# Two of each FFN tile's four weight sums made ahead in DRAM by copies and adding transfers, and loaded

## The chip, the cores and the metric

The kernel runs on one core of a Trainium2 chip. Its time is the device time of one execution in microseconds, as the median of several runs. The engines are named as in the profile: PE is TensorE (matmuls, with PEld for its weight loads), DVE is VectorE, ACT is ScalarE, POOL is GpSimd, SP is the engine that issues most DMA transfers.

## The reference

A trunk of two layers on 512 tokens with D = 1024. Layer 0 mixes with HGRN2 (a gated linear recurrence, evaluated in chunks), then one shared key and value are projected, and layer 1 mixes with chunked band attention. Each mixer is followed by a SwiGLU FFN with 2816 hidden columns. The shift, scale and gate of each step come from a conditioning vector c. The parts that matter here:

```
mod = c_act @ mod_w[layer] + mod_b[layer]
sh1, sc1, g1, sh2, sc2, g2 = jnp.split(mod, N_MOD, axis=-1)
...
u = modulate(rms_norm(h, norm_ffn[layer]), sh2, sc2)
gate, up = jnp.split(u @ w_in, 2, axis=-1)
h = h + g2[:, None, :] * ((jax.nn.silu(gate) * up) @ w_out)
```

## The kernel before, in words

**Numbers.** Everything is fp32. A product of two fp32 matrices is made as three matmuls on halves: each operand is split into a high part (a rounded copy, made on ACT) and a low part (operand minus high part, on DVE); high·high, high·low and low·high are added up in PSUM (mm3, L203 to L205). The low part of a weight is sometimes made by an adding transfer of POOL instead (L144).

**Weights.** `weight_plan` lists all weight pieces, mostly 512 KB, in the order of use. `load` (L159) issues them on SP into three buffers called raw, two pieces ahead of use; `split` (L130) makes the halves, `take` (L192) hands a raw piece out unsplit. Loads on SP are issued in program order, and one that waits for its buffer holds back those behind it.

**The fast tiles.** The FFN's inner columns are 22 tiles of 128 gate and 128 up columns. Tiles 0 to 3 are plain matmuls. Tiles 4 to 21 of both layers go through `fast_tiles` (L532): the 2×2 block product (inner index in even and odd k-tiles, tokens in halves of 256, gate beside up) is made with seven products instead of eight, each of 4 k-tiles × 3 matmuls, so 84 matmuls of 128x256 a tile, on L575 to L577. Their left operands are sums of the weight blocks. The blocks come in two loads, c1 with b11 and b21, c2 with b22 and b12. `prepare(n)` (L544) makes on DVE t1 = b12 − b11 (L554), t2 = b22 − t1 (L555), t3 = b22 − b12 (L558) and t4 = b21 − t2 (L559), in the tiles x1 (t2, t1) and x2 (t3, t4). `halves` (L537) splits them: ACT makes the high part (L540), DVE the low one (L541), for w1 (from c1), w2 (x1), w3 (x2) and w4 (b22 alone). In the profile the loads are `r_f_c`, the sums `f_x`, the halves `f_w_h` and `f_w_l`, the products `f_r`. The preparation of a tile runs while PE works on the tile before it. In tiles 8, 12, 16 and 20, and 4, w4 stands shifted in its buffer.

The input sums, on the tokens' side, are made once per layer in `fast_inputs` (L398 to L414). The seven products are combined on ACT and DVE (L598 to L617) into gate and up, and their product `f_ar` is the tile's result. Later it is split for the output projection (L491/L492 in layer 0, L650/L652 and L687/L688 in layer 1), into places that become free; a list `room` sets which.

**Beside them.** `mod_vectors` (L328) makes the modulation vectors as row reductions on DVE: 512 KB loads `mw` (L342), one instruction L353 each, woven into the mixers and into two of three fast tiles. On POOL stand a few instructions of the normalizations, `ors` (L1095) of the HGRN mixer among them, whose results its chain of DVE and PE waits for; kq (L990) and oe (L1101) are DVE's steps in that mixer that PE waits for.

**Order.** Each engine works through its own list in order; the list of each is laid out when the kernel is built, and places in SBUF that are used again make the waits.

Of the kernel before, what the change touches and what calls it, by code (L numbers as in the profile page):

```python
# [41 lines left out]


FAST = (0, 1)
PLAIN = 4


CUT, MEAN_AT, WRITE_AT = 256, 5, 11
# [26 lines left out]
def trunk(ctx: ExitStack, tc: tile.TileContext, d, out):  # L75
# [295 lines left out]
    def fast_inputs(fp, rb, a, sh, nm):  # L371

        H = S // 2
        his = [fp.tile([P, 8, H], F32R, tag=f"uo{j}", name=f"{nm}_h{j}") for j in range(KT // 2)]
        los = [[cst.tile([P, 2, H], F32R, tag=f"u{'hl'[q % 2]}{2 * j + q // 2}", name=f"{nm}_l{j}_{q}", bufs=1)
                for q in range(4)] for j in range(KT // 2)]
        xs = [fp.tile([P, 4, 2, H], F32, tag=f"xs{g}", name=f"{nm}_x{g}") for g in range(2)]
        ss = [fp.tile([P, 4, 2, H], F32, tag=f"xs{2 + g}", name=f"{nm}_s{g}") for g in range(2)]  # L380

        s1 = cst.tile([P, KT // 2], F32, tag=f"{nm}_sh1", name=f"{nm}_sh1")
        sp = sh.rearrange("p (j e) -> p j e", e=2)
        V.tensor_add(s1, sp[:, :, 0], sp[:, :, 1])
# [12 lines left out]

        def sums(g, late):  # L398
            x, y = xs[g], ss[g]
            if not late:  # L400
                V.tensor_add(y[:, 0], x[:, 0], x[:, 2])
                V.tensor_sub(y[:, 1], y[:, 0], x[:, 1])
                for j in (2 * g, 2 * g + 1):
                    for q, b in ((0, s1[:, j:j + 1]), (1, sh[:, 2 * j + 1:2 * j + 2])):
# [5 lines left out]
            V.tensor_sub(y[:, 3], x[:, 3], y[:, 1])  # L410
            for j in (2 * g, 2 * g + 1):
                v, u_ = y[:, 2:4, j % 2, :], his[j][:, 6:8, :]
                A.activation(u_, v, AF.Copy)
                V.tensor_sub(los[j][3], v, u_)  # L414

        return his, los, sums

    def ffn(layer, z0, u, g2, side, finish):
        nm = f"f{layer}"
        fast = layer in FAST  # L420
        with tc.tile_pool(name=nm, bufs=1) as fp:
# [3 lines left out]
            if fast:  # L425
                his, los, sums = fast_inputs(fp, *u, nm)

                def slot(j, s):
# [2 lines left out]
                u = [(his[k // 2][:, 2 * (k % 2):2 * (k % 2) + 2, :].rearrange("p a c -> p (a c)"),  # L431
                      los[k // 2][k % 2].rearrange("p a c -> p (a c)")) for k in range(KT)]

            def activated(n):

                if not fast or n == FT - 1:
                    return sm.tile([P, S], F32, tag="sq", name=f"{nm}_at{n}", bufs=2)

                g, e = divmod(n, 2) if n < FIRST else divmod(n - FIRST, 4)
                if e == 0:  # L440
                    tag, m = (f"ab{g}", 2) if n < FIRST else (f"xs{g}", 4)
                    raw_a[n] = fp.tile([P, m, S], F32, tag=tag, name=f"{nm}_ar{n}")
                return raw_a[n - e][:, e, :]
# [4 lines left out]
            for n in range(PLAIN if fast else FT):  # L448
                sg = sm.tile([P, S], F32, tag="ut", name=f"{nm}_s{n}", bufs=2)
                at = activated(n)  # L450
                if n == 0:
                    (tg, bg), (tu, bu) = z0
                    A.activation(sg, tg, AF.Silu, bias=bg)
                    V.scalar_tensor_tensor(at, tu, bu, sg, op0=ALU.add, op1=ALU.mult)
                else:
                    res = []
                    drain(proj((nm, n, 0), u, res))
                    if not fast:
                        next(side, None)
# [7 lines left out]
                    V.tensor_mul(at, res[1], sg)  # L467
                kept(n, at)
                if fast and n in (1, 2):
                    sums(0, n == 2)  # L470
            if fast:
                fast_tiles(fp, nm, slot, activated, kept, side)
            if layer == OUT:
                drain(side)
                fast_out(fp, nm, a, raw_a, FIRST, g2, finish)
# [53 lines left out]
                    later = finish(n, c)  # L529
            drain(side)  # L530

    def fast_tiles(fp, nm, slot, activated, kept, side):  # L532

        H = S // 2
        ops = {}
# [1 line left out]
        def halves(key, raw, n_, at=NEAR):  # L537
# [3 lines left out]
            V.tensor_sub(wl, raw, wh)  # L541
            return [(wh[:, i], wl[:, i]) for i in range(n_)]

        def prepare(n):  # L544
# [4 lines left out]
            x1 = fp.tile([P, 2, 4, P], F32, tag="x1", name=f"{m}_x1")  # L549
            x2 = fp.tile([P, 2, 4, P], F32, tag="x2", name=f"{m}_x2")  # L550
# [3 lines left out]
            V.tensor_sub(t1, b12, b11)  # L554
            V.tensor_sub(t2, b22, t1)  # L555
            yield
            ops[n, 6], ops[n, 5] = halves(f"{m}_w2", x1, 2)
            V.tensor_sub(t3, b22, b12)  # L558
            V.tensor_sub(t4, b21, t2)  # L559
            yield  # L560
            ops[n, 7], ops[n, 4] = halves(f"{m}_w3", x2, 2)
            yield
            ops[n, 3], = halves(f"{m}_w4", c2[:, 0:1], 1, NEAR if (n - PLAIN) % EVERY else APART)
            yield
# [64 lines left out]
    def fast_out(fp, nm, a, raw_a, first, g2, finish):  # L629
# [3 lines left out]
        K0 = 2 * PAIRS  # L633
        halves = (slice(0, CUT), slice(CUT, S))
        room = [(cst, f"ul{i}", 1) for i in range(8)] + [(cst, "uh4", 1), (cst, "uh5", 1)]
        room = [(fp, f"sp{i}", 1) for i in range(10)] + room + [(fp, "sp10", 1), (cst, "uh6", 1), (cst, "uh7", 1)]
        room += [(mp, "mraw", 2), (mp, "mraw", 2), (mp, "crow", 2), (fp, "xs1", 4), (fp, "xs0", 4), (sm, "et", 1)]
        units = []

# [124 lines left out]
                T.matmul(ps, wl[:, j, :], uh, start=False, stop=j == PAIRS - 1, skip_group_check=True)  # L764

        def onto(n, c, ps):
            g = ng2 if n % 2 else g2
            V.scalar_tensor_tensor(h[n][:, c], ps, g[:, n:n + 1], h[n][:, c], op0=ALU.mult, op1=ALU.add)

        ng2 = cst.tile([P, KT], F32, tag="a_kv", name="ng2")  # L770
# [53 lines left out]
        for c, ns in zip(halves, (HELD[::-1], HELD)):  # L824
            for n in ns:
                ps = bank(f"{nm}_o{n}_{c.start}h")
                for ci in range(2):
                    for kt in range(CHUNK):
# [993 lines left out]
```

## Time and profile before

| what | value |
|---|---|
| median of 3 runs | 1219.13 us (1218.88 to 1219.14) |
| the profiled execution | 1219.44 us, its span 1217.7 us |
| granted TensorE clock | 0.999 |
| DMA, mean over the span | 151 GB/s, 183.62 MB |
| fast tiles, first matmuls of tile 4 and of the tile after 21 | layer 0 about 340 to 514 us, layer 1 about 920 to 1094 us |

How to read the rows: a row of a group has line, engine, operation, out<-in with buffer numbers left out, shapes and count, then busy us and mean ns of one, then the idle time of the engine just ahead of it and what ended it. A row of a timeline begins with start and duration in us; square brackets hold idle time ahead of it and what ended it. Busy matmuls are pipelined, so the distance of two starts, not the duration, is what one costs. The layer 0 mixer fills about 100 to 300 us, the attention about 640 to 880 us.

### The profile page before, as it was taken

Reading aid. Unit: us, or ns where it says so; the run is one execution under the profiler, and the core shown is the slowest. Engines: PE = TensorE matmul, PEld = TensorE weight load, DVE = VectorE, ACT = ScalarE, POOL = GpSimd, SP = SyncE. Lnnn points to the kernel's source line nnn. Section 1 sums busy time; section 2 is a strip of 40 time slices with the busy share of each in tenths; the row PEclk is TensorE's granted clock in tenths of the full one; section 3 lists DMA queues with packets and bytes.
Section 4 is the critical chain, followed back from the end, with each engine's and each line's share of the span. In section 5 each row is a group of like instructions: output and inputs, shape, how many; then the busy total and the mean of one; then the engine's idle time right before and its main releaser. Section 6 shows DMA issues by size and latency. Waiting matters only on the chain.

```text
span 1217.7 us, 22201 instructions
## 1 busy us (share of the span) xinstructions
PE 1200.7 (99%) x8758; PEld 1052.3 (86%) x8758; DVE 1027.6 (84%) x1860; ACT 668.7 (55%) x1194; POOL 32.0 (3%) x41
## 2 busy tenths in 40 slices
PE   8999999999999999999999999999999999999997
PEld 7887788788899999988888877777889999998997
DVE  8997778977989999987668879996797999988985
ACT  6455446343656666742228556675465566665452
POOL 0100000000000000000000000000000000001100
PEclk9999999999999999999999999999999999999999
DMA  9632354463424444468752444431333344346842
GB/s 358 255 128 98 111 185 150 154 217 121 108 101 139 156 153 143 155 205 278 239 179 83 135 139 138 160 132 36 121 87 121 122 153 148 118 115 155 218 122 91
DMA packets 55992, 183.62 MB, mean 151 GB/s; under 512 B 6352, under 2 KB 8784, under 8 KB 55888
## 3 DMA queue, kind: packets, MB, share of 16 engines
q1 hardware_dynamic: 53584, 175.65, 42.6%
q0 software_dynamic: 2304, 6.55, 3.2%
q8 instruction: 68, 1.11, 0.4%
q14 instruction: 36, 0.29, 0.1%
HBM read 176.68 MB, written 2.10 MB: 147 GB/s over the span
## 4 chain that ended last, share of the span: by engine, by line
PE 84%; DVE 8%; ACT 3%; issue 2%; DMA 2%; POOL 0%; DVEq 0%; POOLq 0%; ACTq 0%
PE f_r L577 9%; PE f_r L575 9%; PE f_r L576 9%; PE f_o L204 4%; PE f_o L205 4%; PE f_o L203 3%; PE f_or L764 1%; PE o L1087 1%; PE f_or L762 1%; PE f_or L763 1%; PE bo L1499 1%; PE bo L203 1%; PE av L226 1%; PE f L205 1%; PE bo L205 1%
## 5 line engine op out<-in xcount | busy, mean ns | idle before, releaser
L577 PE MATMUL f_r<-f_h,f_w_l 128*128 128x256 f32 x1008 | 279.2, 277 | 0.5 <-DVE f_w_l L541 0.5
L575 PE MATMUL f_r<-f_h,f_w_h 128*128 128x256 f32 x1008 | 279.2, 277 | 0.1
L576 PE MATMUL f_r<-f_l,f_w_h 128*128 128x256 f32 x1008 | 279.0, 277 | 0.0
L577 PEld LDWEIGHTS f_r<-f_h,f_w_l 128*128 128x128 f32 x1008 | 189.3, 188 | 0.9 <-DVE f_w_l L541 0.9
L576 PEld LDWEIGHTS f_r<-f_l,f_w_h 128*128 128x128 f32 x1008 | 189.7, 188 | 0.1
L575 PEld LDWEIGHTS f_r<-f_h,f_w_h 128*128 128x128 f32 x1008 | 189.3, 188 | 0.4 <-ACT f_pu L603 0.3
L353 DVE SCALAR_TENSOR_TENSOR mw<-mw,crow 128x1024 f32<-128x1024 f32 x96 | 115.5, 1220 | 0.5 <-DMA mw<-in_modw 0.5
L540 ACT ACTIVATE f_w_h<-f_x 128x1024 fp32r<-128x1024 f32 x72 | 76.8, 1066 | 45.9 <-PE f_r L576 38.9
L541 DVE TENSOR_TENSOR f_w_l<-f_x,f_w_h 128x1024 fp32r<-128x1024 f32 x72 | 88.0, 1224 | 5.9 <-ACT f_w_h L540 3.2
L540 ACT ACTIVATE f_w_h<-r_f_c 128x1024 fp32r<-128x1024 f32 x72 | 61.2, 849 | 42.4 <-PE f_r L576 39.8
L139 ACT ACTIVATE f_o_h<-r_f_o 128x1024 fp32r<-128x1024 f32 (+2 forms) x39 | 34.4, 892 | 77.0 <-PE f_o L204 56.7
L541 DVE TENSOR_TENSOR f_w_l<-r_f_c,f_w_h 128x1024 fp32r<-128x1024 f32 x72 | 68.7, 954 | 6.0 <-ACT f_w_h L540 6.0
L204 PE MATMUL f_o<-f_p,f_o_h 128*128 128x512 f32 x176 | 68.6, 390 | 0.2 <-DVE f_p L492 0.2
L205 PE MATMUL f_o<-f_p,f_o_l 128*128 128x512 f32 x176 | 68.7, 390 | 0.0
L203 PE MATMUL f_o<-f_p,f_o_h 128*128 128x512 f32 x176 | 68.4, 389 | 0.0
L146 DVE TENSOR_TENSOR f_o_l<-r_f_o,f_o_h 128x1024 fp32r<-128x1024 f32 (+2 forms) x35 | 36.1, 1036 | 21.2 <-ACT f_o_h L139 20.0
L1474 ACT ACTIVATE sb<-sb,st 128x128 f32<-128x128 f32 (+1 forms) x64 | 35.9, 561 | 29.9 <-DVE st L1473 29.4
L204 PEld LDWEIGHTS f_o<-f_p,f_o_h 128*128 128x128 f32 x176 | 33.0, 188 | 7.4 <-DVE f_p L492 0.6
L205 PEld LDWEIGHTS f_o<-f_p,f_o_l 128*128 128x128 f32 x176 | 33.0, 188 | 7.3 <-DVE f_o_l L146 0.6
L203 PEld LDWEIGHTS f_o<-f_p,f_o_h 128*128 128x128 f32 x176 | 33.0, 188 | 6.8
L990 DVE TENSOR_TENSOR kq<-kq,t 128x1024 f32<-128x1024 f32 x28 | 34.2, 1223 | 5.1 <-PE fine L1014 2.4
L205 PE MATMUL f<-f_h,f_l 128*128 128x512 f32 x96 | 36.9, 391 | 0.3 <-DMA f_l<-r_f 0.3
(515 smaller groups left out, 3216.2 us busy)
## 6 DMA issues: line engine op xcount, KB each, us to landing
mw<-in_modw SPq DMA_DIRECT2D x96, 512.0 KB, 4.2
r_f_c<-in_ffn_in SPq DMA_DIRECT2D x72, 512.0 KB, 3.3
mrow<-in_modw SPq DMA_DIRECT2D x16, 512.0 KB, 8.1
r_f<-in_ffn_in SPq DMA_DIRECT2D x16, 512.0 KB, 3.3
r_f_o<-in_ffn_out SPq DMA_DIRECT2D x16, 512.0 KB, 3.9
r_f_o<-in_ffn_out SPq DMA_DIRECT2D x16, 320.0 KB, 3.0
r_f_o_c<-in_ffn_out SPq DMA_DIRECT2D x12, 384.0 KB, 4.0
r_av<-in_a_v SPq DMA_DIRECT2D x8, 512.0 KB, 3.9
```

Source lines behind the costliest of these rows:

```text
L139: A.activation(wh, raw, AF.Copy)
L146: low = V.tensor_sub(wl, raw, wh)
L203: T.matmul(ps, wh[:, kt, :], uh, start=start, stop=False)
L204: T.matmul(ps, wh[:, kt, :], ul, start=False, stop=False)
L205: T.matmul(ps, wl[:, kt, :], uh, start=False, stop=stop)
L353: V.scalar_tensor_tensor(mw, mw, 1.0, crow, op0=ALU.mult, op1=ALU.mult, accum_out=raw[:, j:j + 1])
L540: A.activation(wh, raw, AF.Copy)
L541: V.tensor_sub(wl, raw, wh)
L575: T.matmul(ps, wh[:, j, :], uh, start=f, stop=False, skip_group_check=True)
L576: T.matmul(ps, wh[:, j, :], ul, start=False, stop=False, skip_group_check=True)
L577: T.matmul(ps, wl[:, j, :], uh, start=False, stop=stop and j == 3, skip_group_check=True)
L1474: A.activation(s[:, 0:n], s[:, 0:n], AF.Exp, bias=st[:, 1:2], accum_out=st[:, 2:3])
```

## The change

A pool in DRAM is added, and a generator `add_up` that makes two sums per fast tile there: b11 + b12 and b22 + b12. For every two tiles SP copies b11 (then b22) of both from the weights to the new place, 512 KB from DRAM to DRAM, and POOL adds b12 of both onto it with an adding transfer, issued one copy later. One copy goes out with two of three weight loads, from the first load of the gates in layer 0 and of the queries in layer 1 on; 18 copies and 18 adds per layer. In the fast tiles each sum is loaded (256 KB) to where t1 and t3 stood, one tile ahead; even tiles use the places sp0 and sp1, odd ones x1 and x2. DVE makes t2 and t4 only. As the sums have plus signs, t1 and t2 turn their sign against before, and with them the second column and row of the block product: the input sums change signs, and so do the gate g2 in the output (or its negative is used) and the results of the plain tiles. Since sp0 and sp1 are now taken in the fast tiles, the lists of places for the split results are rearranged. Matmuls are the same, one for one, in the same order.

```diff
+    dp = ctx.enter_context(tc.tile_pool(name="dp", bufs=1, space=bass.MemoryType.DRAM))
...
             key, src, nk, n_ = plan[state["loaded"]]
+            for layer, name in enumerate(("g", "bq")):
+                if key[0] == name and layer not in adding:
+                    adding[layer] = add_up(layer)
+            if state["loaded"] % 3:
+                for layer in adding:
+                    next(adding[layer], None)
...
+    def add_up(layer):
+        last = None
+        for b in range(FT - PLAIN)[::BATCH]:
+            for i in range(2):
+                t = dp.tile([P, BATCH, 4 * P], F32, tag=f"t{layer}{b}{i}", name=f"ws{layer}_{b}_{i}")
+                w = d["ffn_in"][layer, PLAIN + b:PLAIN + b + BATCH].rearrange("n v p k c -> v p n (k c)")
+                with tc.issue_after(state["asked"].ins):
+                    nc.sync.dma_start(t, w[i, :, :, 0:4 * P])
+                for e in range(BATCH):
+                    sums_at[layer, PLAIN + b + e, i] = t[:, e, :]
+                if last:
+                    G.dma_start(out=last[0], in_=last[1], accum_op=ALU.add)
+                last = t, w[1, :, :, 4 * P:8 * P]
+                yield
+        G.dma_start(out=last[0], in_=last[1], accum_op=ALU.add)
...
+            if fast and layer != OUT:
+                V.tensor_scalar_mul(g2, g2, -1.0)
...
+                    if fast:
+                        V.tensor_scalar_mul(at, at, -1.0)
...
+        def summed(n):
+            for k in (n, n + 1):
+                if k < FT and k not in asked:
+                    x = [fp.tile([P, 2, 4, P], F32, tag=(f"x{i + 1}", f"sp{i}")[k % 2 == 0], name=f"{nm}_{k}_x{i + 1}") for i in range(2)]
+                    for i in range(2):
+                        nc.sync.dma_start(x[i][:, 1 - i].rearrange("p j c -> p (j c)"), sums_at[layer, k, i])
+                    asked[k] = x
+            return asked.pop(n)
...
-            V.tensor_sub(t1, b12, b11)
-            V.tensor_sub(t2, b22, t1)
+            V.tensor_add(t2, b22, t1)
             yield
             ops[n, 6], ops[n, 5] = halves(f"{m}_w2", x1, 2)
-            V.tensor_sub(t3, b22, b12)
-            V.tensor_sub(t4, b21, t2)
+            V.tensor_add(t4, b21, t2)
...
-        room = [(fp, f"sp{i}", 1) for i in range(10)] + room + [(fp, "sp10", 1), (cst, "uh6", 1), (cst, "uh7", 1)]
+        room = [(fp, f"sp{i}", 1) for i in range(2, 9)] + [(fp, "sp0", 2), (fp, "sp1", 2)] + room + [(cst, "uh6", 1), (cst, "uh7", 1)]
```

On DVE, in layer 1 while PE works on tile 6 (`f_6`: halves of tile 6, `f_7_x`: sums of tile 7), there stands before:

```order
L541 TENSOR_TENSOR f_6_w_l<-f_6_x_9908,f_6_w_h 128x1024
L617 TENSOR_TENSOR f_ar_9693<-f_ar_9693,f_qu_9842 128x256
L554 TENSOR_TENSOR f_7_x_10037<-r_f_7_c_9906,r_f_7_c_9904 128x512
L541 TENSOR_TENSOR f_6_w_l<-f_6_x_9909,f_6_w_h 128x1024
L555 TENSOR_TENSOR f_7_x_10037<-r_f_7_c_9906,f_7_x_10037 128x512
L558 TENSOR_TENSOR f_7_x_10038<-r_f_7_c_9906 128x512
L559 TENSOR_TENSOR f_7_x_10038<-r_f_7_c_9904,f_7_x_10037 128x512
L541 TENSOR_TENSOR f_6_w_l<-r_f_6_c_9780,f_6_w_h 128x512
```

And after, at the same place (L577 is the old L541, L601 and L604 the two sums left):

```order
L577 TENSOR_TENSOR f_6_w_l<-f_6_x_9903,f_6_w_h 128x1024
L577 TENSOR_TENSOR f_6_w_l<-f_6_x_9904,f_6_w_h 128x1024
L662 TENSOR_TENSOR f_ar_9810<-f_ar_9810,f_qu_9963 128x256
L601 TENSOR_TENSOR f_7_x_10029<-r_f_7_c_10027,f_7_x_10029 128x512
L604 TENSOR_TENSOR f_7_x_10030<-r_f_7_c_10025,f_7_x_10029 128x512
L577 TENSOR_TENSOR f_6_w_l<-r_f_6_c_9901,f_6_w_h 128x512
```

Two sums are gone, and the low half of tile 6's w3 (`f_6_w_l<-f_6_x_9904`) no longer stands behind a sum that reads tile 7's c2.

On POOL, in the HGRN mixer, there is before only this around the first two normalizations:

```order
L1337 MEMSET ad 128x1024
L973 MEMSET af_1384 128x256
L1095 TENSOR_TENSOR ors_1294<-oms_1292,nhalf 128x8
L973 MEMSET af_1889 128x256
L1095 TENSOR_TENSOR ors_1805<-oms_1803,nhalf 128x8
```

And after, with the adds (`ws_0_0` is the first sum of tiles 4 and 5, `ws_0_1` the second):

```order
L1382 MEMSET ad 128x1024
L188 DMA ws_0_0_1358<-in_ffn_in 256x1x512
L1018 MEMSET af_1388 128x256
L188 DMA ws_0_1_1597<-in_ffn_in 256x1x512
L1140 TENSOR_TENSOR ors_1296<-oms_1294,nhalf 128x8
L188 DMA ws_2_0_1716<-in_ffn_in 256x1x512
L188 DMA ws_2_1_1877<-in_ffn_in 256x1x512
L1018 MEMSET af_1902 128x256
L188 DMA ws_4_0_1988<-in_ffn_in 256x1x512
L1140 TENSOR_TENSOR ors_1815<-oms_1813,nhalf 128x8
```

Each normalization now stands behind adds, and each add waits for its copy.

On SP, in the second half of that mixer (`mw` are the loads for the row reductions, `r_ao` those of the output projection), there stands before:

```order
L342 DMA mw_0_2270<-in_modw 128x1024
L342 DMA mw_1_2334<-in_modw 128x1024
L342 DMA mw_2_2357<-in_modw 128x1024
L342 DMA mw_3_2453<-in_modw 128x1024
L342 DMA mw_4_2641<-in_modw 128x1024
L164 DMA r_ao_2647<-in_a_out 128x1024
L164 DMA r_ao_2742<-in_a_out 128x1024
L342 DMA mw_5_2730<-in_modw 128x1024
```

And after:

```order
L184 DMA ws_8_0_2672<-in_ffn_in 256x1x512
L368 DMA mw_0_2289<-in_modw 128x1024
L368 DMA mw_1_2356<-in_modw 128x1024
L368 DMA mw_2_2379<-in_modw 128x1024
L368 DMA mw_3_2475<-in_modw 128x1024
L368 DMA mw_4_2666<-in_modw 128x1024
L171 DMA r_ao_2675<-in_a_out 128x1024
L171 DMA r_ao_2770<-in_a_out 128x1024
L184 DMA ws_8_1_2884<-in_ffn_in 256x1x512
L368 DMA mw_5_2758<-in_modw 128x1024
```

Two copies (`ws`) have come in between, each ahead of a load that one of DVE's reductions waits for.

More of the change, by code (lines that the diff above doesn't have):

```diff
@@ L44 @@
 FAST = (0, 1)
-PLAIN = 4
+PLAIN, BATCH = 4, 2
 CUT, MEAN_AT, WRITE_AT = 256, 5, 11
@@ L165, in load @@
             state["loaded"] += 1
+    sums_at, adding = {}, {}
+    def add_up(layer):
[13 more added lines that the diff above has]
+        G.dma_start(out=last[0], in_=last[1], accum_op=ALU.add)
     def fetch(i, ahead):
@@ L382, in fast_inputs @@
         s1 = cst.tile([P, KT // 2], F32, tag=f"{nm}_sh1", name=f"{nm}_sh1")
+        s2 = sm.tile([P, KT], F32, tag="lbt", name=f"{nm}_sh2")[:, 0:KT // 2]
         sp = sh.rearrange("p (j e) -> p j e", e=2)
-        V.tensor_add(s1, sp[:, :, 0], sp[:, :, 1])
+        V.tensor_sub(s1, sp[:, :, 1], sp[:, :, 0])
+        V.tensor_scalar_mul(s2, sp[:, :, 1], -1.0)
         for k in range(KT):
@@ L400, in sums @@
             if not late:
-                V.tensor_add(y[:, 0], x[:, 0], x[:, 2])
-                V.tensor_sub(y[:, 1], y[:, 0], x[:, 1])
+                V.tensor_sub(y[:, 0], x[:, 2], x[:, 0])
+                V.scalar_tensor_tensor(y[:, 1], y[:, 0], -1.0, x[:, 1], op0=ALU.mult, op1=ALU.subtract)
                 for j in (2 * g, 2 * g + 1):
-                    for q, b in ((0, s1[:, j:j + 1]), (1, sh[:, 2 * j + 1:2 * j + 2])):
+                    for q, b in ((0, s1[:, j:j + 1]), (1, s2[:, j:j + 1])):
                         v, u_ = y[:, q, j % 2, :], his[j][:, 4 + q, :]
@@ L409, in sums @@
             V.tensor_sub(y[:, 2], x[:, 1], x[:, 0])
-            V.tensor_sub(y[:, 3], x[:, 3], y[:, 1])
+            V.scalar_tensor_tensor(y[:, 3], x[:, 3], -1.0, y[:, 1], op0=ALU.mult, op1=ALU.subtract)
             for j in (2 * g, 2 * g + 1):
@@ L466, in ffn @@
                     A.activation(sg, res[0], AF.Silu)
-                    V.tensor_mul(at, res[1], sg)
+                    if fast:
+                        V.scalar_tensor_tensor(at, res[1], -1.0, sg, op0=ALU.mult, op1=ALU.mult)
+                    else:
+                        V.tensor_mul(at, res[1], sg)
                 kept(n, at)
@@ L471, in ffn @@
             if fast:
-                fast_tiles(fp, nm, slot, activated, kept, side)
+                fast_tiles(fp, nm, layer, slot, activated, kept, side)
             if layer == OUT:
@@ L530, in ffn, with fast_tiles @@
             drain(side)
-    def fast_tiles(fp, nm, slot, activated, kept, side):
+    def fast_tiles(fp, nm, layer, slot, activated, kept, side):
         H = S // 2
@@ L542, in halves @@
             return [(wh[:, i], wl[:, i]) for i in range(n_)]
+        asked = {}
+        def summed(n):
[6 more added lines that the diff above has]
+            return asked.pop(n)
         def prepare(n):
@@ L548, in prepare @@
             c2 = take((nm, n, "c2")).rearrange("p (o j) c -> p o j c", o=2)
-            x1 = fp.tile([P, 2, 4, P], F32, tag="x1", name=f"{m}_x1")
-            x2 = fp.tile([P, 2, 4, P], F32, tag="x2", name=f"{m}_x2")
+            x1, x2 = summed(n)
             b11, b21, b22, b12 = c1[:, 0], c1[:, 1], c2[:, 0], c2[:, 1]
@@ L766, in onto @@
         def onto(n, c, ps):
-            g = ng2 if n % 2 else g2
+            g = g2 if n % 2 else ng2
             V.scalar_tensor_tensor(h[n][:, c], ps, g[:, n:n + 1], h[n][:, c], op0=ALU.mult, op1=ALU.add)
@@ L784, in fast_out @@
         for n, ps in enumerate(pss):
-            residual(n, ps, g2)
+            residual(n, ps, ng2)
         for n in range(2, HELD[0]):
@@ L796, in fast_out @@
                         ahead((kt + 1) // 2)
-            residual(n, ps, g2)
+            residual(n, ps, ng2)
             if n == MOVED[0]:
@@ L833, in fast_out @@
                         mm3(ps[:, c], ws[n][ci], kt, [x[:, c] for x in a[k]], k == K0, k == FT - 1)
-                residual(n, ps, g2, c)
+                residual(n, ps, ng2, c)
                 later = finish(n, c) or later
```

## The prediction

> **What bounds the kernel now.** I read the page's busy shares first, then its chain, then the rows of the fast tiles, because the change is made for them.
>
> ```profile
> PE 1200.7 (99%) x8758; PEld 1052.3 (86%) x8758; DVE 1027.6 (84%) x1860; ACT 668.7 (55%) x1194; POOL 32.0 (3%) x41
> PE 84%; DVE 8%; ACT 3%; issue 2%; DMA 2%; POOL 0%; DVEq 0%; POOLq 0%; ACTq 0%
> ```
>
> PE is busy for 1200.7 of 1217.7 us and carries 84% of the chain. The change leaves PE's instructions as they are, one for one, so it can only win what PE loses now by waiting or by running slowly. VectorE (DVE), which the change relieves, is second with 84%. The stretches of 20 us in the fast tiles show how near it comes (columns: PE, weight loads, DVE, ACT, POOL, granted clock, DMA share, GB/s):
>
> ```profile
> 380.00:400.00 20.00, 20.00 (x178) 20.00 (x178) 18.87 (x30) 12.41 (x23) 0.00 (x0) 1.00 0.40 137
> 940.00:960.00 20.00, 19.53 (x168) 19.33 (x167) 17.74 (x29) 11.56 (x22) 0.00 (x0) 1.00 0.39 126
> ```
>
> In the first, DVE works 18.87 of 20 us and PE never stops: a full DVE costs nothing as long as it keeps up. Only the second has a hole, of 0.47 us. The list of all that PE waited for says how few holes there are (total us, times, longest):
>
> ```profile
> PE l L1067 <- DVE kq L990: 1.1, 1, 1.1
> PE ot L1110 <- DVE oe L1101: 0.7, 1, 0.7
> PE f_r L577 <- DVE f_w_l L541: 0.5, 1, 0.5
> ```
>
> The first two belong to the HGRN mixer, only the third to the fast tiles: 0.5 us in 3024 matmuls. But PE can be busy and late. Each fast tile is 84 matmuls, so its length is the distance between the starts of its first matmul and of the next tile's. From PE's timeline, the starts of tiles 8, 9, 10, 14, 15 of layer 0, then of tiles 6, 7, 8, 9, 18, 19 of layer 1:
>
> ```profile
> 378.91 0.28 PE L575 MATMUL f_r<-f_h,f_w_h 128*128 128x256 f32 x1
> 388.53 0.28 PE L575 MATMUL f_r<-f_h,f_w_h 128*128 128x256 f32 x1
> 398.05 0.28 PE L575 MATMUL f_r<-f_h,f_w_h 128*128 128x256 f32 x1
> 436.22 0.28 PE L575 MATMUL f_r<-f_h,f_w_h 128*128 128x256 f32 x1
> 446.05 0.28 PE L575 MATMUL f_r<-f_h,f_w_h 128*128 128x256 f32 x1
> ...
> 939.66 0.28 PE L575 MATMUL f_r<-f_h,f_w_h 128*128 128x256 f32 x1
> 950.02 0.28 PE L575 MATMUL f_r<-f_h,f_w_h 128*128 128x256 f32 x1
> 959.91 0.28 PE L575 MATMUL f_r<-f_h,f_w_h 128*128 128x256 f32 x1
> 969.76 0.28 PE L575 MATMUL f_r<-f_h,f_w_h 128*128 128x256 f32 x1
> 1055.71 0.28 PE L575 MATMUL f_r<-f_h,f_w_h 128*128 128x256 f32 x1
> 1065.61 0.28 PE L575 MATMUL f_r<-f_h,f_w_h 128*128 128x256 f32 x1
> ```
>
> An undisturbed tile takes 9.52 us (388.53 to 398.05), one with the shifted w4 9.62 (378.91 to 388.53). Tile 14 of layer 0 takes 9.83. In layer 1 tile 6 takes 10.36, tile 7 9.89, tile 8, which has a shifted w4, 9.85, and tile 18 9.90. So tile 6 stalls, and after it PE goes on at a slower pace, without a hole, until tile 8 is over.
>
> **The change part by part.** It takes t1 and t3 from DVE:
>
> ```profile
> L554 DVE TENSOR_TENSOR f_x<-r_f_c,r_f_c x36: 683/689/693, 334.6 to 1078.0; 128x512 f32<-128x512 f32 x36
> L558 DVE TENSOR_TENSOR f_x<-r_f_c x36: 683/685/691, 335.2 to 1078.7; 128x512 f32<-128x512 f32 x36
> ```
>
> That is 72 × 0.69 = 49 us of DVE's time. Nearly all of it lies beside PE's work, so the gain is not 49 but what the slow tiles lose. Tile 6 of layer 1 shows whether t1 and t3 are on that path:
>
> ```profile
> 943.03 0.69 DVE L554 TENSOR_TENSOR f_x<-r_f_c,r_f_c 128x512 f32<-128x512 f32 x1 [1.92 <-DMA r_f_c<-in_ffn_in]
> 943.64 1.22 DVE L541 TENSOR_TENSOR f_w_l<-f_x,f_w_h 128x1024 fp32r<-128x1024 f32 x1
> ...
> 946.58 0.69 DVE L541 TENSOR_TENSOR f_w_l<-r_f_c,f_w_h 128x512 fp32r<-128x512 f32 x1
> ```
>
> DVE stands 1.92 us for c2 of tile 7, although w3's low half of tile 6 (943.64), which needs no DMA, stands behind that sum. Then come the other sums, and the low half of w4 starts only at 946.58; PE's wait row above names this line. Without t1 and t3 two steps of about 0.60 us (943.03 to 943.64) fall out ahead of it, 1.2 us against a stall of 0.84 (10.36 − 9.52), so the stall goes. The order of after also puts w3's low half ahead of the wait. Next late there is then c2's landing itself, whose sums keep about 0.4 us to spare. With the stall goes the slow pace behind it: tile 7 0.37 (9.89 − 9.52), tile 8 0.23 (9.85 − 9.62). Layer 1 sum: **1.44 us**.
>
> Tile 14 of layer 0 loses 0.31 (9.83 − 9.52). A product split L492 stands there among DVE's rows; it moves to tile 21, since its place sp0 now holds sums, and the two sums ahead go too: **0.31 us**. Tile 18 of layer 1 I leave as it is, since its delay begins on ACT:
>
> ```profile
> 1059.63 0.42 ACT L688 ACTIVATE f_u<-f_ar 128x256 fp32r<-128x256 f32 x1 [0.61 <-DVE mw L353]
> ```
>
> This copy waits for the row reduction L353, and it and another stand ahead of w4's high half on ACT; neither changes its place. The moved splits, three in each layer, each with a copy on ACT like this one:
>
> ```profile
> L491 ACT ACTIVATE f_p<-f_ar x21: 615/623/635, 317.7 to 531.6; 128x512 fp32r<-128x512 f32 x21
> ```
>
> In tiles 20 and 21 their 0.62 us on ACT and 0.69 on DVE cost at least 0, since DVE has two sums less per tile there, and at most one stall like tile 14's in each layer, 0.6 in all; I take 0. The sign turns add one 128x512 multiplication per layer, 0.69 at most like L558, in the plain tiles, hidden by PE: 0, or 0.7 each without that cover.
>
> Then the transfers: 36 copies and 36 adds from DRAM to DRAM, and 72 loads of 256 KB. Before has none of the first two. The nearest rows (KB each, us from issue to landing) and the densest stretch of the HGRN mixer:
>
> ```profile
> mw<-in_modw SPq DMA_DIRECT2D x96, 512.0 KB, 4.2
> r_f_c<-in_ffn_in SPq DMA_DIRECT2D x72, 512.0 KB, 3.3
> f_l<-r_f POOLq DMA_DIRECT2D x4, 512.0 KB, 5.1
> f_t<-in_ffn_out POOLq DMA_DIRECT2D x8, 384.0 KB, 6.7
> ...
> 220.00:250.00 30.00, 28.24 (x371) 22.73 (x371) 24.41 (x38) 13.87 (x39) 1.64 (x1) 1.00 0.55 191
> ```
>
> An add lands after 5.1 (into SBUF) to perhaps 13.4 us (twice the slowest row); I take 6.7, the row with a DRAM addend. The first two adds stand on POOL ahead of the first normalization, and tile 4 first uses their sums where L554 begins now, at 334.6:
>
> ```profile
> 121.70 1.64 POOL L1095 TENSOR_TENSOR ors<-oms,nhalf 128x8 f32<-128x8 f32 x1 [15.26 <-DVE oms L1093]
> ```
>
> So a late add is covered by some 200 us. What is not covered is `ors` behind an add that waits for its copy: POOL is idle 15.26 us before it, the copy ahead of the second add lands in that time; 0, at most the 1.64 of another such instruction. What a copy takes from other transfers: 191 GB/s at a share of 0.55 is 347 GB/s for full engines, so 524288 bytes hold all of them 1.5 us; an add, which reads two and writes one, at most 3.0. In the mixers the weights have two buffers of look-ahead, about 20 us; that covers both. The row reductions' loads have less: 15 of the 36 copies stand on SP directly ahead of one. Now:
>
> ```profile
> L353 DVE SCALAR_TENSOR_TENSOR mw<-mw,crow 128x1024 f32<-128x1024 f32 x96 | 115.5, 1220 | 0.5 <-DMA mw<-in_modw 0.5
> ```
>
> DVE waited 0.5 us for all 96. I take as much again, **+0.5 us**, passed to PE in full; lower end 0 (DVE is idle 5.6 of the 30 us above), upper end in the first rival. By the Trainium skill's page "DMA: Bandwidth & Descriptors", section "Anatomy of one DMA — SWDGE (gpsimd) path", a transfer has about 2.0 us fixed and bytes/436e3 on top, an estimate of 3.2 us for a copy and 1.2 of it on the engines; with that the cost would be 0.4 instead of 0.5. No run here shows a copy from DRAM to DRAM.
>
> In the fast tiles the two sums are asked for one tile ahead, before c1 and c2, when the low halves of w2 and w3 are out; they wait about a tile for their use, and c2 is still the last to land. Cost 0; if they were last, up to 1.9 us per tile as at 943.03.
>
> Sum against the profiled execution of 1219.44: − 1.44 − 0.31 + 0.5 = −1.25, so 1218.2. That execution stands 0.31 above the median of 1219.13, so **1217.9**.
>
> **The rivals.** *Slower: copies in front of the reductions' loads.* DVE takes its instructions in order; an L353 whose load comes late holds back kq (L990) and oe (L1101), the two tiles that PE already waited for. Eight such copies lie in layer 0's mixer. At 1.5 us each they hold DVE 12 us; if half reaches PE, 6.0 − 1.75 = +4.25, or 1223.4. It decides from three copies that reach PE in full: 4.5 − 1.75 = +2.75. For it: the share of 0.55 there. Against it: DVE has waited for these loads once in 96, and has 20% idle. In a sentence of its own: the Trainium skill's page "DMA: Bandwidth & Descriptors", section "Issuing engines are not separate DMA queues", says that transfers of all issuing engines run on the same 16 engines and interleave, so by it the GpSimd adds are no cheaper for these loads than copies on SP; the trace has POOL's 512 KB at 5.1 beside SP's at 3.3, but no two of them together. With the adds as well it would be up to twice, 1229. Chance 0.22.
>
> *No relief: c2 decides.* If c2 lands as late as at 943.03 and its own two sums still make w4 late, the stalls stay where they are or move: 1219.1 to 1219.6 with the 0.5. Against it: the 1.2 us that fall out. Also here: the sums are so early or late that nothing is saved. Chance 0.12.
>
> *More than the stalls.* Tile 4 of both layers also runs slowly (layer 0):
>
> ```profile
> 340.51 0.28 PE L575 MATMUL f_r<-f_h,f_w_h 128*128 128x256 f32 x1
> 350.35 0.28 PE L575 MATMUL f_r<-f_h,f_w_h 128*128 128x256 f32 x1
> ```
>
> 9.84 instead of 9.52. If an earlier start of the preparation cures that in both layers (0.64), tile 18 as well (0.38), and the transfers are free: −1.75 − 1.02 = −2.77, or 1216.4. For it: DVE's queue is shorter in all of them. Against it: tile 4 has no hole. Chance 0.22.
>
> **How the numbers follow.** The forecast itself, 1217.9, has 0.44. A difference of 0.2%, 2.4 us, is about what a measurement of this kernel can tell from no change: forecast and second rival (and a little of the others) lie inside it, 0.56; the third rival gives faster 0.22; the first slower 0.22. The range runs from 1216.1, a little below the third rival, to 1221.9, the first rival with three copies, and leaves out the rest of that rival.
>
> **What would show it.** Right: tiles 6, 7 and 8 of layer 1 at 9.52, 9.52 and 9.62, tile 14 of layer 0 at 9.52, DVE at about 16.4 of 20 us in the fast tiles (18.87 less two sums of 0.60 in 2.1 tiles), waits for r_f_c now in front of L601, and PE's waits in the HGRN mixer within 0.5 of now. Wrong: DVE waits for mw of several us at 110 to 290, or a POOL instruction `ors` that stands behind an add whose copy is late; a stall in another fast tile with a slow pace behind it (0.35 a tile until the next shifted w4); or waits for the new x tiles.

## The result and the profile after

The changed kernel takes 1228.21 us (median of 4 runs, 1227.62 to 1228.55), the one before 1219.14 in the same comparison: a ratio of 1.0074, 95% interval 1.0056 to 1.0091. It is slower by 9.1 us, and 1217.9 with a range to 1221.9 was forecast.

The page of after, its busy shares, the queues, the row reductions and the issues that answer to those shown of before (issues: KB each, us from issue to landing):

```profile
PE 1203.9 (98%) x8758; PEld 1054.5 (86%) x8758; DVE 993.6 (81%) x1793; ACT 667.7 (54%) x1194; POOL 70.1 (6%) x77
...
q1 hardware_dynamic: 73744, 213.41, 51.5%
q0 software_dynamic: 12096, 25.43, 12.8%
...
L379 DVE SCALAR_TENSOR_TENSOR mw<-mw,crow 128x1024 f32<-128x1024 f32 x96 | 115.5, 1218 | 8.4 <-DMA mw<-in_modw 8.2
...
mw<-in_modw SPq DMA_DIRECT2D x96, 512.0 KB, 4.8
r_f_c<-in_ffn_in SPq DMA_DIRECT2D x72, 512.0 KB, 3.8
ws<-in_ffn_in SPq DMA_DIRECT2D x36, 512.0 KB, 6.0
ws<-in_ffn_in POOLq DMA_DIRECT2D x36, 512.0 KB, 8.2
```

DVE has 34 us less to do, and yet the span is 9 us longer: PE stands idle for 22.8 us of it instead of 17.0, and is busy 3.2 us longer. DVE now waits 8.2 us for the reductions' loads, against 0.5. The queues give the transfers' price. On q0 the share rose from 3.2% of 1217.7 us to 12.8% of 1226.7, so 118 us of all 16 engines for 36 adds, 3.3 each. On q1 the time rose by 113 us; the 72 loads of sums, 18.9 MB at what before paid per MB (518.7 us for 175.65 MB), account for 56 of it, the 36 copies for 57, 1.6 each.

First matmuls of tiles of after, from PE's timeline: tile 4 of layer 0; tiles 14 and 15 of it; tiles 6, 7, 8, 9 and 18, 19, 20, 21 of layer 1:

```profile
349.58 0.28 PE L620 MATMUL f_r<-f_h,f_w_h 128*128 128x256 f32 x1
445.29 0.28 PE L620 MATMUL f_r<-f_h,f_w_h 128*128 128x256 f32 x1
454.81 0.28 PE L620 MATMUL f_r<-f_h,f_w_h 128*128 128x256 f32 x1
948.59 0.28 PE L620 MATMUL f_r<-f_h,f_w_h 128*128 128x256 f32 x1
958.11 0.28 PE L620 MATMUL f_r<-f_h,f_w_h 128*128 128x256 f32 x1
967.63 0.28 PE L620 MATMUL f_r<-f_h,f_w_h 128*128 128x256 f32 x1
977.25 0.28 PE L620 MATMUL f_r<-f_h,f_w_h 128*128 128x256 f32 x1
1063.20 0.28 PE L620 MATMUL f_r<-f_h,f_w_h 128*128 128x256 f32 x1
1073.25 0.28 PE L620 MATMUL f_r<-f_h,f_w_h 128*128 128x256 f32 x1
1083.14 0.28 PE L620 MATMUL f_r<-f_h,f_w_h 128*128 128x256 f32 x1
1092.98 0.28 PE L620 MATMUL f_r<-f_h,f_w_h 128*128 128x256 f32 x1
```

The tiles of the forecast did what it said: tile 14 takes 9.52, tiles 6, 7 and 8 take 9.52, 9.52 and 9.62. Tile 18 still stalls, and here the slow pace follows it through tiles 19 and 20 (10.05, 9.89, 9.84), which takes 0.75 back. So of the 1.75 us forecast the fast tiles brought 0.3 in layer 0 and 0.7 in layer 1. But tile 4 of layer 0 starts at 349.58 instead of 340.51: **9.07 us are lost before the first fast tile**. What PE waited for in after (total us, times, longest; ahead of these rows stands one of 3.6, `crow`, at the program's start, which is 3.5 in before):

```profile
PE g L231 <- issue: 2.3, 1, 2.3
PE ao L231 <- DVE ao_l L147: 2.2, 1, 2.2
PE ot L1155 <- DVE oe L1146: 2.1, 3, 0.9
PE l L1112 <- DVE kq L1035: 1.1, 1, 1.1
```

Two holes are new, and one has grown. PE's instructions are the same in both kernels, so for each one its start in before can be subtracted from its start in after. The difference rises to 3.0 us by PE's instruction that starts at 224 in before, in steps of 0.1 to 1.1 us; by 2.46 at the hole of g; and by 4.1 from the hole of ao on. About 0.5 is won back ahead of tile 4, 0.3 of it where before itself waits for an adding transfer.

Two of the small steps, 1.1 and 0.4 us, are the forecast's first rival at the place it named: DVE waits for `mw`, the normalization and oe come late, and PE waits for oe. (A third, 0.6 us at 144.64, is a hole of the kind of g's.) The larger of the two, on DVE and then on PE:

```profile
206.66 1.23 DVE L379 SCALAR_TENSOR_TENSOR mw<-mw,crow 128x1024 f32<-128x1024 f32 x1 [1.55 <-DMA mw<-in_modw]
211.84 0.63 PE L1155 MATMUL ot<-ident,oe 128*128 128x128 f32 x4 [0.95 <-DVE oe L1146]
```

The hole of ao is the same rival at another place. DVE's timeline of after, with the wait at 266.73, then PE's clock in some stretches of 1 to 2 us (columns as before: PE, weight loads, DVE, ACT, POOL, granted clock, DMA share, GB/s):

```profile
263.43 0.08 DVE L379 DVE_READ_ACCUMULATOR mw<-mw,crow 128x1 f32 x1
266.73 1.23 DVE L379 SCALAR_TENSOR_TENSOR mw<-mw,crow 128x1024 f32<-128x1024 f32 x1 [3.22 <-DMA mw<-in_modw]
```

```profile
273.00:275.00 2.00, 0.00 (x0) 0.00 (x0) 2.00 (x4) 1.68 (x3) 0.00 (x0) 1.00 0.16 66
275.00:276.00 1.00, 0.97 (x4) 0.79 (x5) 1.00 (x2) 0.00 (x0) 0.00 (x0) 0.83 0.00 0
276.00:277.00 1.00, 1.00 (x4) 0.81 (x3) 1.00 (x2) 0.00 (x0) 0.00 (x0) 0.50 0.85 250
...
278.00:279.00 1.00, 1.00 (x4) 0.72 (x4) 1.00 (x2) 0.71 (x2) 0.00 (x0) 0.50 0.86 254
...
280.00:281.00 1.00, 1.00 (x6) 0.84 (x5) 0.00 (x0) 0.00 (x0) 0.00 (x0) 1.00 1.08 381
```

DVE stands 3.22 us for a load; the low half of an output weight (ao_l) stands behind it, and PE stops for 2.2 us. Shortly after PE goes on, its granted clock is 0.50 for 3.4 us, so the hole costs nearly as much again: 2.36 us and then 1.74. The Trainium skill's page "TensorE: Matmul & The Clock Gate", section "Part 1: The HAM clock gate (the "warmup" mystery)", describes this half-rate state and a free-running window of about 3.4 us, and puts the fall to it after at least one idle window; here a hole of 2.2 us was enough, so the measurement is the stricter rule.

The traces of all runs together (e1 to e12 are the experiments below) say when it falls. Within a trace the granted clock changes only at whole steps of 3.41 us (in after 78 steps at 1.00, then 1 at 0.50, then 276 at 1.00). Between 100 and 345 us seven such steps at full clock had PE idle for 2.03 us or more (2.18 in after, 2.71 and 2.80 in e4, 2.64 in e5, 2.70 in e10, 2.03 in e11, 2.78 in e12), and after each of them the next step ran at 0.50. No step at full clock with 1.48 us of idle time or less did that to the next. So it counts where a hole lies on this grid: the 2.31 us at g in after fall into two steps, 0.83 and 1.48, and the clock stays. Between 1.48 and 2.03 us nothing was measured.

The first hole has no visible cause in the list of waits. PE's row, and the DMA queues of after in the quarter of a microsecond from 230.25 (packets, MB, share of 16 engines):

```profile
232.76 0.50 PE L231 MATMUL g<-u0h,g_l 128*128 128x512 f32 x1 [2.31 <-issue]
```

```profile
q1 hardware_dynamic: 46, 0.09, 97.0%
q8 instruction: 1, 0.02, 22.0%
```

Queue q8, which the profile calls "instruction", carries a part of the program, a packet at a time. This packet starts at 230.45, among engines that are full with other transfers; PE goes on 2.3 us later. In before the packet starts at 224.64, on nearly idle engines, and the same matmul runs at 227.30 without a hole, 2.7 us later. The packet itself is no slower in after (0.88 us of one engine, 22.0% of 16 engines in a quarter of a microsecond, against 1.17): it starts late.

### The profile page after: what moved, and what is told of

Same layout as the page of the kernel before. It is cut to its first block, busy times and chain, and to the rows that moved or that the text cites. A ratio compares the mean times of both kernels' runs of the same rounds, so it can differ in the third digit from the quotient of the medians.

```text
span 1226.7 us, 22421 instructions
## 1 busy us (share of the span) xinstructions
PE 1203.9 (98%) x8758; PEld 1054.5 (86%) x8758; DVE 993.6 (81%) x1793; ACT 667.7 (54%) x1194; POOL 70.1 (6%) x77
## 3 DMA queue, kind: packets, MB, share of 16 engines
q0 software_dynamic: 12096, 25.43, 12.8%
## 4 chain that ended last, share of the span: by engine, by line
PE 69%; DVE 9%; ACT 3%; DMA 3%; issue 2%; POOL 0%; DVEq 0%; POOLq 0%; ACTq 0%; SPq 0%
PE f_r L620 9%; PE f_r L621 9%; PE f_r L622 9%; PE f_o L230 3%; PE f_o L231 3%; PE f_o L229 3%; PE f L229 2%; PE f L231 2%; PE f L230 2%; DMA mw<-in_modw 2%; DVE mw L379 1%; PE f_or L809 1%; PE f_or L807 1%; PE f_or L808 1%; PE bo L1544 1%
## 5 line engine op out<-in xcount | busy, mean ns | idle before, releaser
L577 DVE TENSOR_TENSOR f_w_l<-f_x,f_w_h 128x1024 fp32r<-128x1024 f32 x72 | 88.2, 1225 | 9.0 <-ACT f_w_h L576 4.6
L577 DVE TENSOR_TENSOR f_w_l<-r_f_c,f_w_h 128x1024 fp32r<-128x1024 f32 x72 | 68.8, 956 | 30.9 <-ACT f_w_h L576 30.8
L188 POOL DMA_DIRECT2D ws<-in_ffn_in x34 | 36.0, 1059 | 350.7 <-DMA ws<-in_ffn_in 350.7
```

The costliest lines, as they stand in the source:

```text
L188: G.dma_start(out=last[0], in_=last[1], accum_op=ALU.add)
```

## The experiments

They ran on three chips, beside runs of before of their own (medians 1219.8 to 1219.9, single executions 1217.4 to 1223.4), so the place of loss is read from the start of layer 0's tile 4, 340.51 in before. A trace shows one execution, in e5 and e11 it is one near the upper end of the scatter (1228.61 of 1223.60 to 1230.11; 1223.82 of 1219.78 to 1223.83). Kernels that leave out transfers or sums do not compute the whole result; e3, e4 and e7 do.

**e1, no transfers.** `sums_at[...] = d["ffn_in"][layer, k, i]` instead of the copy and the add.

> The changed kernel without its 36 copies and 36 adds; the tiles load b11 and b22 themselves (256 KB each, straight from the weights) where the sums would be, so b12 is left out of these sums. Order, signs, loads and DVE's relief are as after. Theory (the transfers' traffic is the loss, about 9.1 us in front of layer 0's first fast tile): that tile starts near 340.5 again instead of 349.6, the fast tiles keep their gain of 0.3 in layer 0 and 0.7 in layer 1, the output stage its loss of about 0.8: 1218.4 to 1219.3. Rival (the loads of the sums or the changed order cost it): 1226 or more.

Measured: 1218.66, ratio 0.9983 (0.9972 to 0.9993); tile 4 starts at 340.21. The loss belongs to the copies and adds alone. The loads of the sums and the changed order cost nothing there.

**e2, copies only.**

```diff
-                if last:
-                    G.dma_start(out=last[0], in_=last[1], accum_op=ALU.add)
...
-        G.dma_start(out=last[0], in_=last[1], accum_op=ALU.add)
```

> The changed kernel with its 36 copies but without the 36 adds (b12 is left out of the sums). Theory (the 16 engines are taken up, 1.6 us of all of them by a copy and 3.3 us by an add, from the shares of the queues): the loss shrinks to a third or less, 1219 to 1222. Rival 1 (copies standing on SP ahead of the reductions' loads are the loss): it stays, 1225 or more. Rival 2 (POOL's adds make the normalizations wait): no loss is left, 1218.4 to 1219.3.

Measured: 1220.75, ratio 1.0002 (0.9988 to 1.0016); tile 4 at 341.04. Of the 9.07 us 0.53 are left; a small hole at g alone is 0.7. So copies in front of the reductions' loads, the first rival's mechanism as it was priced, are not enough.

**e3 and e4, one layer each.** `if layer == 1` (or 0) around the copies and loads; in the other layer DVE makes t1 = b11 + b12 and t3 = b22 + b12.

> Sums from DRAM in layer 1 alone; in layer 0 DVE makes all four sums again (with the signs turned), and there are no copies and adds in the HGRN mixer. Theory (all of the loss comes from the transfers in the HGRN mixer): 1219.1 - 0.7 (fast tiles of layer 1) + 0.2 to 0.9 (attention and output stage) = 1218.6 to 1219.5. Rival (transfers beside the attention cost about half): 1222 to 1225.

> Sums from DRAM in layer 0 alone; in layer 1 DVE makes all four sums. Theory: 1219.1 + 9.1 - 0.3 = 1227.9, plus up to 0.8 in the output stage if its rearranged places cost that: 1227.5 to 1229. Rival (half of the loss belongs to layer 1): 1222 to 1225.

Measured: e3 1219.82, ratio 0.9996 (0.9985 to 1.0007); e4 1230.49, ratio 1.0073 (1.0050 to 1.0097), tile 4 at 351.99. The loss is layer 0's: beside the attention the same transfers cost 0.2 to 0.5 us (from tile 21's end to layer 1's tile 4 before takes 407.4 us, after 407.6, e3 407.9). Both times lie a little above what was expected, e4's by 1.5 us. e4 showed something else: tiles 6, 7, 8 of layer 1 ran at 9.52, 9.52, 9.62 although DVE made all four sums there.

**e5 and e6, holes in the transfers.** `if (layer, b, i) in ((0, 8, 1),):`, in e6 `((0, 10, 1), (0, 12, 0))`: no copy and add for these.

> After, with one copy and its add left out in layer 0 (second sum of tiles 12 and 13, the add that POOL issued at 223.04; those tiles load b22 without b12). Theory (PE's 2.31 us without a visible cause at 230.4, and 3.15 in the layer-0-only run, are a load of PE's own instructions that queues behind this add while the DMA engines are full): the hole of PE at g L231 near 230 is below 0.5 us, the first fast tile starts 2 to 3 us sooner, near 347, and the run takes about 1225.5. Rival (the hole belongs to PE's program or to a wait that the profile does not show, whatever the traffic): 2 to 3 us of hole remain, 1227.5 to 1228.5.

> After, with two copies and their adds left out in layer 0 (second sum of tiles 14 and 15, first of 16 and 17; the adds issued at 257.24 and 263.38, ahead of and beside five loads for the row reductions). Theory (DVE waits 3.22 us at 266.73 for such a load, PE 2.17 us behind it for the low half of an output weight, then 1.7 us more at a lower granted clock): DVE's wait there falls to 0.5 as in the kernel before, PE's to 0, the clock stays at 1.00, and 3.5 to 4.0 us are saved: about 1224.3. Rival (the lateness of the chain ahead makes PE wait there): under 1 us is saved, 1227.3 to 1228.3.

e5: PE's hole at g fell from 2.31 to 0.37, and the median to 1225.86, ratio 1.0056 (1.0034 to 1.0078), both as expected. But tile 4 did not come sooner in the profiled execution, the second slowest of five: it starts at 351.02, as the hole at ao became 3.3 with 6.8 us at half clock behind it, and smaller holes came earlier in the mixer. e6: DVE's wait for mw at that place fell to 0.3 (its longest is 2.1, at 162.89), no hole at ao, the clock at 1.00; tile 4 at 345.27 (4.3 us less than after), 1224.08, ratio 1.0042 (1.0026 to 1.0059), as expected. Its hole at g stayed, 2.58, in two steps of the clock's grid (1.34 and 1.24), without half clock behind it.

**e8, small adds.** `out=last[0][0:8], in_=last[1][0:8]`, so that POOL's order and waits stay and the adds' bytes go.

> After, with each add of both layers cut to 8 of 128 partitions (1/16 of the bytes; the rest of the sums lacks b12); copies, loads, order and POOL's waits for the copies stay. Theory (the adds' traffic): as with copies only, the first fast tile near 341, 1219 to 1220.5. Rival (the normalizations that stand on POOL behind adds that wait for their copies): the loss stays, over 1224.

Measured: 1220.12, ratio 1.0003 (0.9994 to 1.0013); tile 4 at 341.84, of the loss 1.3 left, 1.2 of it the hole at g. So POOL's order is not the loss.

**e10, copies three times.** Two more `nc.sync.dma_start` of each copy to places of their own, no adds.

> Copies only, each issued three times on SP to different places (108 copies, no adds): 3 x 1.6 = 4.8 us of all 16 DMA engines for each copy and add of after (1.6 + 3.3 = 4.9). Theory A (what counts is how long the engines are full, whoever asks): a loss like after's, first fast tile of layer 0 at 346 to 352, 1225 to 1231. Theory B (the adds cost through POOL's software queue and its wait for the copy, not through their engine time): near the run with copies only, first fast tile below 343, 1219 to 1222.

Measured: 1225.17, ratio 1.0044 (1.0029 to 1.0059); tile 4 at 345.77, just under the range of theory A. Plain copies on SP with nearly the same engine time (775 us on q0 and q1 together, 789 in after) cost 5.3 us, so a large loss needs no add and no software queue. It is made of other parts, though: 4.3 of the 5.3 are the hole at g, 2.71 here, and half clock behind it, and the hole at ao did not come. The stretch from 190 to 220 of before, after and e10:

```profile
190.00:220.00 30.00, 30.00 (x292) 24.88 (x290) 26.16 (x44) 16.39 (x40) 1.95 (x2) 1.00 0.49 162
```

```profile
190.00:220.00 30.00, 29.03 (x244) 24.16 (x230) 24.55 (x41) 16.57 (x42) 4.08 (x4) 1.00 0.79 246
```

```profile
190.00:220.00 30.00, 29.82 (x291) 24.69 (x290) 25.53 (x44) 15.96 (x41) 1.95 (x2) 1.00 0.87 285
```

What the adds cost beyond this is not settled: e10 has DVE waiting 1.7 us for mw where after has 8.2.

**e11 and e12, two pairs alone.** As e1, but `if (layer, b, i) not in ((0, 8, 1), (0, 10, 0)):`, in e12 `((0, 10, 1), (0, 12, 0))`.

> After without copies and adds but for two pairs, second sum of tiles 12 and 13 and first of 14 and 15 (in after, add at 223.04 and copy beside PE's hole of 2.31 us at 230.4). Theory: the hole at g L231 near 227 is there again with 1 to 3 us, and nearly nothing else is lost before the fast tiles: first fast tile at 341.5 to 343.5, 1219.5 to 1221.5. Rival (the hole needs the lateness that earlier transfers build up): below 0.5 us of hole, first fast tile at 340.2 to 341, 1218.3 to 1219.3.

> After without copies and adds but for two pairs, second sum of tiles 14 and 15 and first of 16 and 17 (in after, ahead of and beside the five loads behind which DVE waits 3.22 us). Theory: DVE waits 1.5 to 3.5 us for mw near 258, PE 1 to 3 us for ao_l behind it, then 1 to 2 us more at a lower granted clock: first fast tile at 342.5 to 345, 1220.5 to 1223. Rival (it needs the backlog of all the others): below 0.7 us of wait, first fast tile near 340.3, 1218.3 to 1219.3.

Two of 36 pairs of a copy and an add each, and each run brings its hole back. e11: 1222.32, ratio 1.0017 (1.0007 to 1.0026), tile 4 at 344.42. PE's row and its clock there (PE, granted clock, DMA share, GB/s):

```profile
229.86 0.50 PE L240 MATMUL g<-u0h,g_l 128*128 128x512 f32 x1 [2.03 <-issue]
```

```profile
231.00:232.00 1.00, 1.00 (x34) 0.50 0.73 258
232.00:233.00 1.00, 1.00 (x3) 0.50 0.85 277
233.00:234.00 1.00, 1.00 (x4) 0.50 0.79 145
```

The hole of 2.03 us is followed by half clock here, unlike the one of 2.31 in after, since it lies in one step of the clock's grid, and so costs 2.2 + 1.5. e12: 1224.70, ratio 1.0038 (1.0023 to 1.0053), tile 4 at 346.36. Its DVE waits and PE's hole:

```profile
260.87 1.23 DVE L388 SCALAR_TENSOR_TENSOR mw<-mw,crow 128x1024 f32<-128x1024 f32 x1 [2.48 <-DMA mw<-in_modw]
263.76 1.22 DVE L388 SCALAR_TENSOR_TENSOR mw<-mw,crow 128x1024 f32<-128x1024 f32 x1 [1.65 <-DMA mw<-in_modw]
266.52 1.23 DVE L388 SCALAR_TENSOR_TENSOR mw<-mw,crow 128x1024 f32<-128x1024 f32 x1 [0.86 <-DMA mw<-in_modw]
```

```profile
271.00 0.80 PE L240 MATMUL ao<-yq,ao_l 128*128 128x512 f32 x1 [3.24 <-DVE ao_l L147]
```

No backlog of the others is needed: two copies and two adds at a bad place do it. Both cost more than expected: e11 because nothing had been allowed for the clock, e12 because PE's hole is above the 1 to 3 us and 0.6 us more came at 335.81, where PE waits for an adding transfer that before has too.

In all seven runs with a hole of over 0.5 us at g, PE went on 2.3 to 2.4 us after that packet of q8 started (packet to matmul: after 230.45 to 232.76, e2 225.71 to 228.12, e4 230.66 to 233.03, e6 229.92 to 232.34, e8 226.56 to 228.92, e10 229.07 to 231.50, e11 227.59 to 229.86), whatever the hole's length; in e12, without transfers there, the packet came at 225.14 and there was no hole.

The count of instructions settles what the packet is. From 20 us on the traces have 16 holes of PE of over 0.2 us with nothing but "issue" to end them, at g and earlier in the mixer, and each has a q8 packet 2.2 to 2.5 us ahead. In the order of PE's matmuls and weight loads they stand at four places only, numbers 2497, 3521, 3778 and 4802, counted from 0: 1024, 257 and 1024 apart, so multiples of 256 to within one. A q8 packet has 16384 bytes, and 68 of them for 17597 instructions of PE are 259 each. So these holes are PE waiting for the next packet of its own instructions. All 16 are in runs with copies beside them (after, e2, e4, e5, e6, e8, e10, e11); before, e1, e3, e7 and e9 have neither, and in e12 the copies come later. So the transfers make the packet late; where it waits, in the queues or ahead of them, is in no view.

**e7 and e9, the fast tiles' gain taken apart.** e7 is before with the changed list of places; e9 is before without t1 and t3 (zeros stand for them).

```diff
-        room = [(fp, f"sp{i}", 1) for i in range(10)] + room + [(fp, "sp10", 1), (cst, "uh6", 1), (cst, "uh7", 1)]
+        room = [(fp, f"sp{i}", 1) for i in range(2, 9)] + [(fp, "sp0", 2), (fp, "sp1", 2)] + room + [(cst, "uh6", 1), (cst, "uh7", 1)]
```

> The kernel before with one line of the change: the list of places for the output stage's split results (sp0 and sp1 behind sp2 to sp8). All four sums stay on DVE, no transfer is added. It moves a split out of ACT's and w3's low half ahead of the wait in DVE's order at tile 6 of layer 1. Rival that now leads, since tile 6 ran clean in the layer-0-only run with all four sums on DVE: tiles 6, 7, 8 of layer 1 at 9.52, 9.52, 9.62, so up to 1.44 less, 1217.7 to 1218.5. The prediction's theory (the relief of two sums is what removes the stall): tile 6 stays at 10.36, 1219.1.

> The kernel before with t1 and t3 left out (their places hold zeros written once per layer; t2 and t4 are made from them): DVE's relief alone, with the old places, no copies, adds or loads. DVE's wait for c2 of tile 7 still stands between w2's and w3's low half of tile 6. The prediction's theory: 1.2 us fall out ahead of w4's low half, so tiles 6, 7, 8 of layer 1 take 9.52, 9.52, 9.62 and tile 14 of layer 0 9.52. Rival (only the order and the places matter, as in the run with the places alone): tile 6 stays above 10. Either way the time is within 2 us of before, since the output stage may give it back: 1217.5 to 1220.

Starts of tiles 6, 7, 8 of layer 1, in e9 and in e7:

```profile
939.20 0.28 PE L576 MATMUL f_r<-f_h,f_w_h 128*128 128x256 f32 x1
948.72 0.28 PE L576 MATMUL f_r<-f_h,f_w_h 128*128 128x256 f32 x1
958.24 0.28 PE L576 MATMUL f_r<-f_h,f_w_h 128*128 128x256 f32 x1
```

```profile
939.53 0.28 PE L575 MATMUL f_r<-f_h,f_w_h 128*128 128x256 f32 x1
949.05 0.28 PE L575 MATMUL f_r<-f_h,f_w_h 128*128 128x256 f32 x1
958.57 0.28 PE L575 MATMUL f_r<-f_h,f_w_h 128*128 128x256 f32 x1
```

9.52 in both: either cures tile 6. Tile 14 of layer 0 is cured by the relief (9.52 in e9) and not by the places (9.83 in e7). The times do not move: e9 1218.96, ratio 0.9995 (0.9986 to 1.0005); e7 1219.93, ratio 0.9999 (0.9989 to 1.0008). e7 is 1.6 us ahead at the end of the fast tiles and gives that back in the output stage, where PE waits behind a weight that lands late. The rows of PE's wait, of the late weight, and of the adding transfers' queue from 1119 to 1127:

```profile
PE f_or L764 <- DVE f_o_1l L703: 1.2, 1, 1.2
```

```profile
1126.67 0.74 ACT L139 ACTIVATE f_o_h<-r_f_o 128x640 fp32r<-128x640 f32 x1 [2.57 <-DMA r_f_o<-in_ffn_out]
```

```profile
q0 software_dynamic: 334, 0.80, 61.1%
```

Why this weight is late is not shown: adding transfers hold 61.1% of the engines there, but in before they hold 75.2% in the same 8 us, and PE does not wait.

None of the versions with the whole computation beats before by more than the measurement can tell.

## Why the prediction was wrong

**What held.** PE as the bound, and the relief's mechanism: tile 14, and tiles 6 to 8 of layer 1 came out as forecast, and e9 shows that the two sums alone suffice. That they were the only way was wrong (e7). Tile 18 kept its stall, as said; that the slow pace would follow it to tile 20 was not seen, and it took 0.75 of the 1.75 us back. Why it did is open: e9 has it without any transfer, and e1 does not. The transfers' engine time was nearly right: 1.5 and at most 3.0 us of all engines forecast, 1.6 and 3.3 measured. The second estimate there, 3.2 us to landing and 1.2 on the engines, was low: a copy landed after 6.0. DVE's load in the fast tiles of layer 0 (350 to 510 us) fell from 19.0 of 20 us to 17.0, by 2.0 where 2.5 were forecast.

**The step that failed** is "I take as much again, +0.5 us, passed to PE in full". DVE's waits for `mw` rose to 8.2 us instead of 1.0, and 9.07 us were lost before layer 0's first fast tile. The term was scaled from what DVE waited for these loads in before, and not from how full the engines would be. The forecast's own numbers say that: 18 copies and adds at 1.5 + 3.0 are 81 us of full engines, put into the 207 us from the first copy to the last, of which 0.45 was already taken: 0.84. After shows 0.80 over 100 to 307 us, and 0.65 to 0.94 in stretches of 30.

But the mean share is not what decides. Over 110 to 300 us e11 and e12 have 0.50 and 0.49, nearly the 0.47 of before, and lose 3.9 and 5.9 us ahead of tile 4; and from 280 to 310 us PE never stops in after, though these 30 us have the fullest engines:

```profile
280.00:310.00 30.00, 30.00 (x138) 24.98 (x137) 21.48 (x38) 11.20 (x15) 5.20 (x5) 1.00 0.94 250
```

What decides is full engines for some microseconds at a place where something comes without a long lead: 0.94 from 222 to 228 in e11, where PE's instructions are due, and 0.96 and 0.85 from 240 to 260 in e12, ahead of five loads for the reductions. Such loads land after 7.5 us in e12 and 7.9 in after (median of those issued from 252 to 268), against 3.7 in before: a load is late by more than the 1.5 us of one copy.

**The rival that came nearest** was the first. Its mechanism is there (DVE 8.2 us behind mw), but it counted only the copies ahead of such loads, which cost little (e2), and put the adds into a side sentence. The figure of 1229 there, for copies and adds, is near the result by luck: it had no range and no chance of its own, and the loss is made of other parts. Its place was right in part only: PE's waits for oe grew from 0.7 to 2.1 us, those for kq hardly, and the larger loss came at ao_l.

**What no case held.** That PE's own program comes over the same engines: 2.46 of the 9.07 us at g, and 0.6 more at 144.64. That a hole of 2 us can be followed by 3.4 us at half clock: 1.74 in after, 1.5 each in e11 and e12. And the sentence that the weights' look-ahead "covers both" was right for weights and said nothing of what has no look-ahead in the code.

**POOL's order** cost little: only the first normalization stood behind its add. It came 1.85 us later (123.55 instead of 121.70), a little more than the 1.64 allowed, and PE has no hole there. The other three wait for DVE, as before. e8 keeps that order and loses 1.3 us in all.

## What to carry to other kernels

Before moving work from an engine to DMA, add the new transfers' engine time to the share that each short stretch already has, not to a mean over the kernel. Where the sum nears 1, look for the loads that come without a long lead, here the reductions' loads and PE's own instructions, and price their lateness and what stands behind it, not the transfer alone. An adding transfer took about twice the engine time of a plain copy of the same bytes (3.3 against 1.6 us). And ask what a relieved engine was late for: here 49 us of sums were worth 1.0 us net in the fast tiles, and one line of places alone won 1.4 there (e7).

## What the runs showed of the hardware that was not expected

PE's instructions arrive by DMA, 16384 bytes and some 256 instructions at a time (queue q8). In the runs with holes PE went on 2.2 to 2.5 us after a packet started, and in before, without a hole, 2.7 us: there are only a few tenths to spare at g. So full DMA engines can stop PE, at g for 0.4 to 3.2 us, with nothing to see but "issue".

The granted clock changes on a grid of 3.41 us. A step at full clock with 2.03 us or more of idle PE was followed by one at 0.50, one with up to 1.48 was not. So the same hole costs 1.5 to 1.7 us more or nothing more, by where it lies on the grid: 2.03 us in e11 did, 2.31 in after and 2.58 in e6, each split over two steps, did not.
